# First layer of a two-layer trunk: low parts of k written by VectorE, last values projected ahead of the last queries

## The chip, the core and the metric

One core of a Trainium2 chip runs the whole program. The metric is the device time of one execution in microseconds (us). The engines are TensorE (PE, with its weight loads as PEld), VectorE (DVE), ScalarE (ACT) and GpSimd (POOL); SyncE (SP) issues the DMAs.

## The reference, cut to what matters

The trunk has two layers on 512 tokens of width 1024, in float32. Layer 0 mixes with stick-breaking attention, layer 1 with dilated attention; each layer then has a feed-forward block and a gated addition (PLE). Only the first mixer is touched by the change:

```python
q, k, v = jnp.split(x @ w_in, 3, axis=-1)          # 16 heads of 64
for blk in range(S // Q_BLOCK):                      # blocks of 128 queries
    z = einsum('bqhd,bkhd->bhqk', q[:, t0:L], k[:, :L]) * scale
    log_fail = where(past, log_sigmoid(-z), 0.0)
    later = cumsum(log_fail, reverse=True) - log_fail
    a = where(past, exp(log_sigmoid(z) + later), 0.0)
    outs.append(einsum('bhqk,bkhd->bqhd', a, v[:, :L]))
return concatenate(outs) @ w_out
```

## The kernel before

**Precision.** Every product is made of single-pass fp32r matmuls. A value is split into a high part (ScalarE rounds it by a copy) and a low part (VectorE subtracts), and high x high, high x low and low x high are summed. Weights arrive as units of 128 x 1024 (`Weights`, L64 to L118); ScalarE (L100), or GpSimd for every second unit from 6 to 28 (L98), makes the high part and VectorE (L101) the low part.

**Heads.** A pair `pr` of heads (two heads of 64 features) is projected by `queries(pr)` (L466): eight steps of three matmuls for q into one PSUM bank, eight for k into another. `query_part` scales each out of PSUM (L462: `qf`, then `kf`), and after `kf` calls `heads_split` (L368). For head a that makes `qa` (high part of q in partitions 0 to 63, low part in 64 to 127), `ka` (the high part of k in both halves) and `la` (the low part of k in both halves); `qb`, `kb`, `lb` are the same for head b. So one matmul `ka` by `qa` and one `la` by `qa` give all products.

For pairs 2 to 7 (`moved`) whole tiles are split (`qh`, `ql`, `kh`, `kl`: L380, L383, L386, L391), and twelve DMAs of 128 KB, issued one after the other by SP (`move`, L375), carry the halves to their places. For pairs 0 and 1 the engines write the halves themselves, except that the second half of `la` and of `lb` is a copy of the first by DMA (L406).

**Attention of one head n** (0 to 15; `pr = n // 2`). `stage1(n)` (L471) makes the scores in PSUM tile `z` and starts the logarithms on ScalarE and VectorE; its first matmul reads `ka` and `qa` (L478), its third reads `la` (L485). `stage2(n)` (L510) adds the running sums with `sh`, `sl`, `Lh`, `Ll` and starts the exponential `e`, `eh`, `el`. `stage3(n)` (L530) multiplies by the values. There are two `z` tiles and two further PSUM banks (`mm`) for all projections, `stage3` and PLE tiles.

**Order of the work.** TensorE's order is the order in which the program is written; the other engines' orders are planned from priorities. Between the stages `Filler` (L123) deals out projection steps from a queue, each counted as 0.65 on its own clock. Its queue here is, before the change, q2, v1, q3, q4, q5, v2, q6, q7, v3 (`q` is a pair's queries and keys, `v` the values of four heads, 16 steps each, 144 in all), and behind them two PLE tiles of two steps each ("tail"). The loop over n is

```python
stage2(n); fill(share * 0.57)
fill.until(("q", (n + 2) // 2), 5.0)     # pair done, and 5.0 of other steps after it
stage1(n + 2); fill(share * 0.32)
fill.until(("v", n // 4), 0.0); settle(1.5); stage3(n)
if n == 12: fill.add("out3", ...)        # output projection, only now in the queue
fill(share * 0.11)
```

`until` (L149) runs steps until the label is done and the extra 5.0 have passed; if the queue runs empty it stops there. A step of values is six matmuls of 256 columns, one of queries three of 512.

Of the kernel before, what the change touches and what calls it, by code (L numbers as in the profile page):

```python
# [11 lines left out]
F32 = mybir.dt.float32  # L12
# [153 lines left out]
def program(tc, ctx, w_dram, x_dram, xs_dram, p_dram, pos_dram, g_dram, c_dram, out_dram):  # L166
    nc = tc.nc
    pe, act, dve, pool = nc.tensor, nc.scalar, nc.vector, nc.gpsimd
# [10 lines left out]
    def U(name, dt=F32):  # L179
        return up.tile([P, T], dt, name=name, tag="u")  # L180

    def tmp(name, dt=F32):
        return tp.tile([P, T], dt, name=name, tag="tmp")
# [39 lines left out]
    def due(what):  # L223

        return tc.high_priority(offset=-TUNE[what])
# [30 lines left out]
    HALF = (slice(0, 64), slice(64, 128))  # L256
# [108 lines left out]
                            evac(n, ps[n], ALL)  # L365
                    yield 0.65

    def heads_split(qf, kf, name, moved):  # L368


        qa, qb, ka, kb, la, lb = (U(name + s, F32R) for s in ("qa", "qb", "ka", "kb", "la", "lb"))
        a, b = HALF

        def move(dst, src):
            nc.sync.dma_start(dst.bitcast(F32), src.bitcast(F32))  # L375

        with due("hsplit"):
            if moved:
                qh, ql, kh = tmp("qh", F32R), qf.bitcast(F32R), tmp("kh", F32R)
                act.activation(qh, qf, AF.Copy)  # L380
                move(qa[a], qh[a])
                move(qb[b], qh[b])
                dve.tensor_sub(ql, qf, qh.bitcast(F32))  # L383
                move(qa[b], ql[a])
                move(qb[a], ql[b])
                act.activation(kh, kf, AF.Copy)  # L386
                for h, t in ((a, ka), (b, kb)):
                    move(t[a], kh[h])
                    move(t[b], kh[h])
                kl = tmp("kl", F32R)  # L390
                dve.tensor_sub(kl, kf, kh.bitcast(F32))  # L391
                for h, t in ((a, la), (b, lb)):
                    move(t[a], kl[h])
                    move(t[b], kl[h])
            else:
                act.activation(qa[a], qf[a], AF.Copy)
                act.activation(qb[b], qf[b], AF.Copy)
                dve.tensor_sub(qa[b], qf[a], qa[a].bitcast(F32))
                dve.tensor_sub(qb[a], qf[b], qb[b].bitcast(F32))
                act.activation(ka[a], kf[a], AF.Copy)  # L400
                act.activation(kb[b], kf[b], AF.Copy)
                act.activation(ka[b], kf[a], AF.Copy)
                act.activation(kb[a], kf[b], AF.Copy)
                for h, t, k in ((a, la, ka), (b, lb, kb)):
                    dve.tensor_sub(t[h], kf[h], k[h].bitcast(F32))
                    move(t[HALF[1 - HALF.index(h)]], t[h])  # L406
        return (qa, qb), (ka, kb), (la, lb)


    def stick_breaking(xh, xl, sq, oh, ol, tail, tail_prepare, out):  # L410
        with tc.tile_pool(name="sbw", bufs=1, reuse_waits="tile") as wp, \
                tc.tile_pool(name="sbz", bufs=2, space=PSUM, reuse_waits="tile") as zp:
            seg = {0: (0, 512), 1: (512, 384), 3: (896, 128), 2: (1024, 256)}
            vt, norm, qk, live = {}, {}, {}, {}
# [10 lines left out]
            def value_part(qv, t, ps):  # L425
                norm["read"] = fill.clock + 0.65
                c = norm["col"][:, t:t + 1]
                v = wp.tile([P, 4, 2, 64], F32R, name="v", tag="v", bufs=8)
                with due("vev"):
                    src = ps[:, (t % 2) * 256:(t % 2) * 256 + 256].rearrange("p (h d) -> p h d", h=4)  # L430
                    hi, lo = v[:, :, 0], v[:, :, 1]
                    act.activation(hi, src, AF.Copy, scale=c)
                    dve.scalar_tensor_tensor(lo, src, c, hi.bitcast(F32), ALU.mult, ALU.subtract)
                vt[qv, t] = v

            def values(qv):
                w = []
                for t0 in (0, 2):
                    ps = bank()
                    for k in range(KT):  # L440
                        if t0 == 0:
                            w.append(W.take("w_in_sb", k, 2048 + qv * 256, 256))
                        for t in (t0, t0 + 1):
                            value_step(ps, k, t, *w[k])
                        if k == KT - 1:
                            value_part(qv, t0, ps)
                            value_part(qv, t0 + 1, ps)
                        yield 0.65
# [9 lines left out]
            def query_part(pr, f, m, ps):  # L458
                norm["read"] = fill.clock + 0.65
                f[m] = tmp("qf" if m == 0 else "kf")  # L460
                with due("qev"):
                    dve.tensor_mul(f[m], ps, norm["row8"] if m == 0 else norm["row"])  # L462
                if m == 1:
                    qk[pr] = heads_split(f[0], f[1], f"sb{pr}", pr > 1)

            def queries(pr):  # L466
                f = {}
                yield from linear("w_in_sb", [pr * P, 1024 + pr * P], xh, xl,
                                  lambda m, ps, cs: query_part(pr, f, m, ps), bank)
# [94 lines left out]
            for pr in range(2):  # L564
                f = {}
                for m in range(2):
                    query_part(pr, f, m, cols[2 * pr + m])
            for t in range(4):
                value_part(0, t, vps[t // 2])
            for name, n in (("q", 2), ("v", 1), ("q", 3), ("q", 4), ("q", 5), ("v", 2), ("q", 6), ("q", 7),  # L570
                            ("v", 3)):
                fill.add((name, n), queries(n) if name == "q" else values(n))
            fill.done.update({("q", 0): 0.0, ("q", 1): 0.0, ("v", 0): 0.0})
            fill(TUNE["p0"])
# [383 lines left out]
    def layer(i, h, xh, xl, sq, last):  # L958
# [44 lines left out]
        if i == 0:  # L1003
            stick_breaking(xh, xl, sq, oh, ol, [ple_tile(m, bank, U) for m in range(2)], ple_parts, out)
            later["pool"] = ctx.enter_context(tc.tile_pool(name="wide", bufs=6, space=PSUM, reuse_waits="tile"))
        else:
            outs = {}
            dilated(xh, xl, sq, oh, ol, outs, out, ple_parts)
# [158 lines left out]
    h, xh, xl, s = layer(0, xs_dram, xh, xl, s, False)  # L1167
# [45 lines left out]
```

## Time and profile before

| | |
|---|---|
| median of 3 runs | 1430.84 us (1430.02 to 1432.11) |
| the profiled execution | 1431.45 us, span 1429.3 us |
| PE busy | 1401.6 us, 98% of the span |
| DVE, ACT busy | 899.3 us (63%), 643.4 us (45%) |
| chain that ended last | PE 87%, DVE 7%, ACT 4%, issue 1%, DMA 1% |
| layer 0 attention, us 40 to 240 | DVE 15 to 18.5 and ACT 16 to 18 of each 20 us until 200, less after |

The span is the time between the first and last instruction of the profiled execution; its own time is 2.15 us longer. A row of the timeline gives start and duration in us, engine, line, operation and tiles; in square brackets stands the idle time of the engine just before and what ended it. Matmuls overlap, so the distance of two starts is the cost of one, not the duration.

### The profile page before, as it was taken

The page shows a single profiled execution, that of the slowest core. Times are in us where ns is not written, and L with a number is a line of the kernel's source. Part 1 is how long each engine was busy: PE and PEld are TensorE (multiplying, and loading weights), DVE is VectorE, ACT ScalarE, POOL GpSimd, SP SyncE. Part 2 cuts the span into 40 slices and gives each one's busy share as a digit, 9 for nine tenths or more (in the row PEclk, how much of TensorE's full clock was granted, in tenths as well). Part 3 has the DMA queues.
Part 4 walks back from the last instruction along what each step waited for, and adds up shares of the span by engine and source line. Part 5 has one row for each costly group of instructions (what it writes and reads, how often), then busy time and mean ns, then how long its engine had stood idle before and what let it go on. Part 6 is the DMA issues. An engine that isn't in the chain of part 4 may idle for free.

```text
span 1429.3 us, 18374 instructions
## 1 busy us (share of the span) xinstructions
PE 1401.6 (98%) x7218; PEld 1181.3 (83%) x7218; DVE 899.3 (63%) x1503; ACT 643.4 (45%) x1010; POOL 46.1 (3%) x27
## 2 busy tenths in 40 slices
PE   8999999999999999999999999999999999999998
PEld 7888997888888888887988788899888888888877
DVE  4788886485253453548868888866872444535476
ACT  4788986553232221335552525546632322222353
POOL 0111111000000000000000000000000000000000
PEclk9999999999999999999999999999999999999999
DMA  6344452423232323232522212132323333323321
GB/s 207 104 110 120 111 135 67 138 89 103 89 103 89 103 89 102 90 94 73 167 74 89 74 45 75 59 105 88 89 89 101 91 103 89 102 90 96 96 83 65
DMA packets 45270, 138.86 MB, mean 97 GB/s; under 512 B 5696, under 2 KB 6592, under 8 KB 45184
## 3 DMA queue, kind: packets, MB, share of 16 engines
q1 hardware_dynamic: 45104, 137.43, 31.9%
q8 instruction: 57, 0.93, 0.3%
q0 software_dynamic: 80, 0.26, 0.1%
q14 instruction: 29, 0.24, 0.1%
HBM read 123.51 MB, written 4.19 MB: 89 GB/s over the span
## 4 chain that ended last, share of the span: by engine, by line
PE 87%; DVE 7%; ACT 4%; issue 1%; DMA 1%; SPq 0%; ACTq 0%; DVEq 0%
PE wb L358 17%; PE wb L360 17%; PE wb L362 17%; PE mmb L358 5%; PE mmb L362 5%; PE mmb L360 5%; ACT S L774 1%; DVE wlo L101 1%; PE mmb L421 1%; PE mmb L422 1%; PE mmb L423 1%; PE wb L725 1%; PE z L261 1%; PE z L259 1%; PE z L260 1%
## 5 line engine op out<-in xcount | busy, mean ns | idle before, releaser
L100 ACT ACTIVATE whi<-wraw_t 128x1024 fp32r<-128x1024 f32 (+1 forms) x298 | 228.9, 798 | 440.6 <-PE wb L362 345.7
L101 DVE TENSOR_TENSOR wlo<-wraw_t,whi 128x1024 fp32r<-128x1024 f32 (+1 forms) x310 | 276.1, 911 | 238.7 <-ACT whi L100 235.5
L358 PE MATMUL wb<-nh,whi 128*128 128x512 f32 (+1 forms) x594 | 227.4, 385 | 4.4 <-ACT nh L264 4.4
L360 PE MATMUL wb<-nh,wlo 128*128 128x512 f32 (+1 forms) x594 | 226.4, 384 | 0.0
L362 PE MATMUL wb<-nl,whi 128*128 128x512 f32 x576 | 207.7, 391 | 0.4 <-DVE nl L268 0.4
L358 PE MATMUL wb<-fh,whi 128*128 128x512 f32 x496 | 196.5, 396 | 0.0
L360 PE MATMUL wb<-fh,wlo 128*128 128x512 f32 x496 | 196.5, 396 | 0.0
L362 PE MATMUL wb<-fl,whi 128*128 128x512 f32 x496 | 196.5, 396 | 0.0
L358 PEld LDWEIGHTS wb<-nh,whi 128*128 128x128 f32 x594 | 111.7, 188 | 28.8 <-ACT nh L264 7.0
L360 PEld LDWEIGHTS wb<-nh,wlo 128*128 128x128 f32 x594 | 111.7, 188 | 21.6
L362 PEld LDWEIGHTS wb<-nl,whi 128*128 128x128 f32 x576 | 107.8, 188 | 23.3 <-DVE nl L268 1.3
L362 PEld LDWEIGHTS wb<-fl,whi 128*128 128x128 f32 x496 | 93.3, 188 | 22.4
L358 PEld LDWEIGHTS wb<-fh,whi 128*128 128x128 f32 x496 | 93.3, 188 | 22.4
L360 PEld LDWEIGHTS wb<-fh,wlo 128*128 128x128 f32 x496 | 93.3, 188 | 22.4
L358 PE MATMUL mmb<-nh,whi 128*128 128x512 f32 x248 | 100.1, 404 | 0.0
L362 PE MATMUL mmb<-nl,whi 128*128 128x512 f32 x248 | 97.4, 393 | 0.0
L360 PE MATMUL mmb<-nh,wlo 128*128 128x512 f32 x248 | 97.3, 392 | 0.0
L1103 DVE TENSOR_TENSOR f<-wb,f 128x512 f32<-128x512 f32 (+1 forms) x50 | 33.3, 666 | 73.5 <-PE wb L362 71.1
L1078 DVE TENSOR_TENSOR z<-wb,rrow 128x512 f32<-128x512 f32 x60 | 40.5, 686 | 55.8 <-PE wb L362 55.7
L1081 ACT ACTIVATE fh<-z 128x512 fp32r<-128x512 f32 x64 | 39.9, 631 | 77.3 <-DVE z L1079 77.3
L291 DVE TENSOR_TENSOR acc<-acc,sq 128x512 f32<-128x512 f32 (+1 forms) x74 | 48.8, 659 | 15.6 <-ACT sq L287 15.0
L362 PEld LDWEIGHTS mmb<-nl,whi 128*128 128x128 f32 x248 | 46.9, 189 | 10.2
(818 smaller groups left out, 2600.8 us busy)
## 6 DMA issues: line engine op xcount, KB each, us to landing
wraw_t<-w SPq DMA_DIRECT2D x219, 512.0 KB, 3.6
x<-x SPq DMA_DIRECT2D x8, 256.0 KB, 7.1
h<-xs SPq DMA_DIRECT2D x8, 256.0 KB, 5.9
spill<-h SPq DMA_DIRECT2D x8, 256.0 KB, 2.7
h<-spill SPq DMA_DIRECT2D x8, 256.0 KB, 6.5
out<-h SPq DMA_DIRECT2D x7, 256.0 KB, 2.1
praw<-p SPq DMA_DIRECT2D x4, 256.0 KB, 4.2
wraw_t<-w SPq DMA_DIRECT2D x4, 128.0 KB, 3.5
```

The source lines that it names most:

```text
L100: self.highs.append(self.nc.scalar.activation(hi[:, c], src[:, c], AF.Copy))
L101: self.lows.append(self.nc.vector.tensor_sub(lo[:, c], src[:, c], hi[:, c].bitcast(F32)))
L259: pe.matmul(ps, ah, bh, start=start, stop=False, skip_group_check=True)
L260: pe.matmul(ps, ah, bl, start=False, stop=False, skip_group_check=True)
L261: pe.matmul(ps, al, bh, start=False, stop=stop, skip_group_check=True)
L291: self.adder.tensor_tensor(self.acc[:, cs], self.acc[:, cs], self.sq[:, cs], ALU.add)
L358: pe.matmul(ps[m][:, cs], wh, xh[k][:, cs], start=(k == 0 and cs is not TWO[1]), stop=False, skip_group_check=True)
L360: pe.matmul(ps[m][:, cs], wl, xh[k][:, cs], start=False, stop=False, skip_group_check=True)
L362: pe.matmul(ps[m], wh, xl[k], start=False, stop=(k == nk - 1), skip_group_check=True)
L1078: dve.tensor_mul(z, ps, norm["row"])
L1081: act.activation(a, z, AF.Copy)
L1103: dve.tensor_add(y[m][:, cs], ps, y[m][:, cs])
```

## The change

Two edits. For pair 0 VectorE subtracts a second time, straight into the other half of `la` and `lb`, where a DMA copied it. In the Filler's queue the last values (v3) stand ahead of the last pair of queries (q7). Pair 1 keeps its DMAs; nothing else differs.

```diff
-    def heads_split(qf, kf, name, moved):
+    def heads_split(qf, kf, name, moved, at_once):
...
                 for h, t, k in ((a, la, ka), (b, lb, kb)):
                     dve.tensor_sub(t[h], kf[h], k[h].bitcast(F32))
-                    move(t[HALF[1 - HALF.index(h)]], t[h])
+                    other = HALF[1 - HALF.index(h)]
+                    if at_once:
+                        dve.tensor_sub(t[other], kf[h], k[h].bitcast(F32))
+                    else:
+                        move(t[other], t[h])
...
-                    qk[pr] = heads_split(f[0], f[1], f"sb{pr}", pr > 1)
+                    qk[pr] = heads_split(f[0], f[1], f"sb{pr}", pr > 1, pr == 0)
...
-            for name, n in (("q", 2), ("v", 1), ("q", 3), ("q", 4), ("q", 5), ("v", 2), ("q", 6), ("q", 7),
-                            ("v", 3)):
+            for name, n in (("q", 2), ("v", 1), ("q", 3), ("q", 4), ("q", 5), ("v", 2), ("q", 6), ("v", 3),
+                            ("q", 7)):
```

## Rows read from the trace of the kernel before

**Rows 1.** The page, part 1: busy us, share of span, instructions.

```profile
PE 1401.6 (98%) x7218; PEld 1181.3 (83%) x7218; DVE 899.3 (63%) x1503; ACT 643.4 (45%) x1010; POOL 46.1 (3%) x27
```

**Rows 2.** Timeline of PE, first scores of head 0: start, us, instruction, idle.

```profile
51.50 0.39 PE L478 MATMUL z<-sb0qa,sb0ka 128*128 128x512 f32 x1
51.73 0.22 PE L480 MATMUL z<-rconst 128*128 128x128 f32 x1
53.01 0.47 PE L485 MATMUL z<-sb0qa,sb0la 128*128 128x512 f32 x1 [1.06 <-DMA sb0la<-sb0la]
```

**Rows 3.** Timeline of DVE around the low parts of pair 0.

```profile
49.92 0.68 DVE L405 TENSOR_TENSOR sb0la<-kf,sb0ka 64x512 fp32r<-64x512 f32 x1
...
51.36 1.23 DVE L101 TENSOR_TENSOR wlo<-wraw_t,whi 128x1024 fp32r<-128x1024 f32 x1
...
58.99 1.49 DVE L498 SCALAR_TENSOR_TENSOR s<-z,s 128x1280 f32<-128x1280 f32 x1 [1.68 <-ACT s L497]
```

**Rows 4.** Timeline of PE: PLE tiles, stages 3(12), 2(13), 1(15).

```profile
213.91 0.40 PE L358 MATMUL mmb<-ph,whi 128*128 128x512 f32 x1
...
214.61 0.40 PE L358 MATMUL mmb<-ph,whi 128*128 128x512 f32 x1
...
216.78 0.47 PE L358 MATMUL mmb<-ph,whi 128*128 128x512 f32 x1 [1.31 <-DVE v L433]
...
217.81 0.51 PE L538 MATMUL mmb<-eh,v 128*128 128x512 f32 x1
...
219.14 0.44 PE L513 MATMUL z<-sh,rconst 128*128 128x512 f32 x1
...
221.16 0.40 PE L358 MATMUL mmb<-ph,whi 128*128 128x512 f32 x1
...
223.24 0.47 PE L478 MATMUL z<-sb7qb,sb7kb 128*128 128x512 f32 x1
...
224.87 0.45 PE L259 MATMUL out<-o2h,whi 128*128 128x512 f32 x1
```

**Rows 5.** Timeline of PE: first matmul after keys of pairs 2, 6, 7; pair 6 used.

```profile
61.47 0.28 PE L421 MATMUL mmb<-whi,x0h 128*128 128x256 f32 x1
...
176.29 0.40 PE L358 MATMUL mmb<-x0h,whi 128*128 128x512 f32 x1
...
186.50 0.47 PE L485 MATMUL z<-sb6qa,sb6la 128*128 128x512 f32 x1 [0.32 <-DMA sb6la<-kl]
...
195.94 0.28 PE L421 MATMUL mmb<-whi,x0h 128*128 128x256 f32 x1
```

**Rows 6.** View by tile, sb2la and sb7la: DMA issues, first and last start; landing.

```profile
L375 SPq DMA_DIRECT2D sb2la<-kl x2: 540/571/602, 70.3 to 70.9; - x2
...
L375 SPq DMA_DIRECT2D sb7la<-kl x2: 539/563/587, 202.5 to 203.1; - x2
DMA to landing us min/median/max: 2.3/2.4/2.4
```

**Rows 7.** Timeline of DVE: q of pair 7 leaves PSUM.

```profile
185.70 0.68 DVE L462 TENSOR_TENSOR qf<-mmb,row 128x512 f32<-128x512 f32 x1
```

**Rows 8.** Timeline of ACT and SP: pair 7's split begins.

```profile
196.53 0.62 ACT L380 ACTIVATE qh<-qf 128x512 fp32r<-128x512 f32 x1
...
197.17 0.47 SPq L375 DMA_DIRECT2D sb7qa<-qh  x1
```

**Rows 9.** Windows: us, busy of PE, PEld, DVE, ACT, POOL, then granted clock.

```profile
716.00:720.00 4.00, 2.24 (x15) 1.95 (x15) 3.32 (x6) 4.00 (x6) 0.00 (x0) 0.90 0.16 20
720.00:724.00 4.00, 4.00 (x19) 4.00 (x20) 2.72 (x7) 1.72 (x4) 1.83 (x1) 0.50 0.28 111
214.00:218.00 4.00, 2.59 (x11) 1.54 (x10) 1.67 (x3) 3.64 (x5) 2.77 (x1) 1.00 0.35 121
218.00:222.00 4.00, 4.00 (x24) 3.60 (x24) 3.41 (x8) 1.96 (x3) 0.00 (x0) 1.00 0.23 55
```

**Rows 10.** Timeline of DVE: last low part of head 15's sums.

```profile
236.45 0.82 DVE L507 TENSOR_TENSOR Ll<-L,Lh 128x640 fp32r<-128x640 f32 x1
```

## The prediction

> **What bounds the kernel.** I read the page first: TensorE is busy for 98% of the span, no other engine comes near [rows 1], and the chain of waits is TensorE's own work for the most part. So what counts is where TensorE stands still. The list of its waits gives few; in the stretch that the change touches they are short, and the timeline shows each in its place. Three matter. Head 0's first matmul with a low part of k waits 1.06 us for the DMA that copies it [rows 2]. Head 12's waits 0.32 us for a DMA of pair 6 [rows 5]. The second PLE tile waits 1.31 us for VectorE to clear the bank of the last values [rows 4]. A fourth, at about 231 us, is head 14's exponential; it follows stage 2 of head 14 in either order and is left as it is. Then I followed pair 7 from its last key matmul to its use, because that pair is the one moved.
>
> **Edit 1, pair 0.** Removed: two DMAs of SP. Added: two subtractions of 64x512 on VectorE at 0.68 us each, the price of the same operation into the first half [rows 3]. `la` is then complete at 49.92 + 2 x 0.7 = 51.3 us, ahead of 51.9, when TensorE wants it after the two matmuls that precede it [rows 2]. The wait of 1.06 us goes: **-1.1 us**. The ends: 0, if VectorE's plan puts other work between the two halves, and -1.2: the starts stand 1.28 us apart, and 128 columns need a quarter of the 0.23 us that the 512-column matmul ahead took. The added 1.4 us of VectorE push what is queued behind it: the low part of a weight unit at 51.36, then pair 1's split and an eviction. The first to notice would be the logarithm step at 58.99, and VectorE stood idle for 1.68 us before that one, waiting for ScalarE [rows 3]; that idle time covers the 1.4. Without that cover it would cost at most the 1.4. On SP the weight load behind the two copies waits for that same low part, so it starts 1.4 us later; it fetches a unit needed much later. I take 0.
>
> **Edit 2, what it removes.** The queue order decides which 16 steps come last. Stage 2 of head 12 starts after 135 of the 144 steps in either order, since every step counts 0.65 and no `until` before it asks for v3 or q7. Before, the nine left are values: five, stage 1 of head 14, four more, then three PLE steps, the third after the bank wait. That wait vanishes, for the bank is then pair 7's and is cleared by the multiply of L462, planned early, while the first PLE tile runs. From 213.91 two steps at 0.70 end at 215.3, the third began at 216.78 [rows 4]: **-1.5 us** (0 if the multiply is late by two steps). Pair 6 is now followed by nine steps of values before its use, six short matmuls each instead of three long ones and so a little longer; the 0.32 us shrinks: **-0.2 us** (0 to -0.3, the whole wait).
>
> **Edit 2, what it adds.** Stage 1 of head 14 needs pair 7. The nine steps left after stage 2 of head 12 are now pair 7's own, so `until` runs all nine, and then asks for 5.0 of other steps. The queue holds four PLE steps (2.6) and nothing more: the output projection joins it only behind stage 3 of head 12. So `until` stops, and stage 1 of head 14 stands four steps after the last key matmul. On the chip that is 4 x 0.70 = 2.8 us [rows 4], plus 0.4 for the two matmuls ahead of the one that reads `la` [rows 2]: 3.2 us.
>
> What pair 7 needs in that time: `kf` out of PSUM, the rounding on ScalarE, the subtraction on VectorE, and twelve DMAs one behind the other on SP, the tenth of which completes `la`. The trace has this path six times. For pair 7 the keys end at 195.94, the second `la` DMA is issued at 203.1 and lands 2.4 us later: 9.6 us [rows 5, 6]. For pair 6 TensorE itself waited, 10.2 us after the keys [rows 5]. The longest is pair 2: 70.9 + 2.4 - 61.47 = 11.8 us [rows 5, 6]. I take 9.6, the nearest row: the same pair, at a time when ScalarE and VectorE will have less to do than they had then, because TensorE feeds them nothing new. TensorE is in order, and behind the waiting matmul stand stage 3 of head 12, stage 2 of head 13 and the output projection, which could all have run. So it stands still for 9.6 - 3.2 = **+6.4 us** (+8.6 with pair 2's length, +3.8 in the second rival).
>
> **After the stall.** Stage 2 of head 14 now follows its stage 1 by stage 3(12) and stage 2(13), 3.35 us from 217.81 to 221.16, four steps (2.8), stage 1(15) (1.63), two steps (1.4) and stage 3(13) (1.33): 10.5 us [rows 4]. Head 15's last low part was ready at 237.27, 12.4 us after its stage 1 ended at 224.87 [rows 4, 10], and it is read in the last quarter of stage 2, some 1.5 of the 2.0 us from 219.14 to 221.16; so 10.9 is wanted and 10.5 there. I take this as even (0 to +1.5).
>
> **The clock.** Where TensorE was busy for 2.24 of 4 us, the granted clock fell to 0.50 for the next 4 us (1.2 GHz instead of 2.4); around the 1.31 us wait, busy 2.59 of 4, it stayed at 1.00 [rows 9]. A stall of 6.4 us, broken only by two matmuls, is much worse than the first. Four microseconds at half clock lose 2 us: **+2.0 us** (0 to +4, a fall twice as long). What the lower clock loses in stage 1 and 3 is time that ScalarE and VectorE gain for head 14, so it and the term above do not add up in full.
>
> The Trainium skill's page "TensorE: Matmul & The Clock Gate", section "Part 1: The HAM clock gate (the "warmup" mystery)", says that "the default state is throttled, and activity releases the throttle". By that rule the edit costs more than the stall itself, and the sum would hold the clock term; a reading of the 1.31 us wait alone would leave it out. Rows 9 show both outcomes.
>
> **Sum.** -1.1 - 1.5 - 0.2 + 6.4 + 2.0 = +5.6 us. On the profiled execution's 1431.45 that is 1437.05; that execution is 0.61 above the median of the runs shown, and on the median it is 1436.4. I predict 1436.5. Nothing later gives it back, since TensorE bounds the rest too.
>
> **Rivals.**
> - *The stall without the fall of the clock*: +3.6, so 1434.4. For it: no fall after 1.31 us. Against: the fall shown by rows 9 after far less idle time.
> - *The split starts early.* q of pair 7 leaves PSUM long before its keys end. If its rounding and four q DMAs went ahead then, SP would start with k: `kf`, rounding and six DMAs at 0.6, landing at about 7.0, a stall of 3.8 and no fall: +1.0, 1431.9. Against: before, `qf` was there at 185.70, yet `qh` began at 196.53 and the first DMA at 197.17, both after the last key matmul, before 195.94 [rows 5, 7, 8]; the other five pairs show the same order.
> - *Covered: not slower.* If `la` of pair 7 lands within 3.2 us of the keys, the stall is nothing and only the gains stand: -2.8, 1428.0. That decides at one point, the matmul of stage 1 of head 14 that reads `la`. Against: two landings in a row cannot be beaten; 2.4 us of 3.2 are one DMA's landing alone [rows 6].
> - *Pile-up.* The path takes pair 2's 11.8 us, or the clock stays down twice as long, with heads 13 to 15 now bunched on ScalarE: +8 to +10, about 1440. For it: three heads' chains follow one stall.
> - *Edit 1 does nothing*, because the second half of `la` is planned behind the weight unit: 1.1 more on any of these; it moves the time within the range only.
>
> **How the numbers follow.** Forecast 60%, no fall 12%, early split 9%, covered 6%, pile-up 13%. The range is 1432 to 1441: it reaches from the early split to the pile-up's end and leaves out the covered case and what lies beyond a +10. A measurement of this kernel can tell about 0.2%, 2.9 us, from no change; slower by that means above 1433.7. Forecast, no fall and pile-up lie there: 85%. The early split and half of the covered case lie within: 12%. Faster: 3%.
>
> **What would show it.** In the changed kernel's timeline: the first `la` matmul of head 0 under 0.2 us after the one before; no wait of a PLE tile for values; stage 1 of head 14 behind four PLE steps, its first matmul waiting about 4 us for a DMA of `sb7ka` and its third again about 2 us for `sb7la`; a granted clock of 0.50 within a few us of it. The prediction is wrong if those waits together are under 3 us, if TensorE has other steps ahead of stage 1 of head 14, or if head 14's stage 2 waits for longer than 3 us.

## The result, and the profile after

The changed kernel takes 1443.43 us (median of 4 runs, 1442.68 to 1444.0), the kernel before 1431.47 beside it: ratio 1.0083 [1.0066, 1.01], +12.0 us. Forecast were 1436.5 and a range of 1432 to 1441. The sign came as forecast, and so did the stall that was to cause it; the size did not. The profiled execution took 1443.91, 12.46 more than that of before; its span is 12.5 longer. Of the eleven runs of e6 below one took 2801.06 us, for a reason that no run here shows, and it is left out of e6's figures.

The page, part 1: every engine is busy as before within 0.5%, so the 12 us are time in which TensorE stands still or runs slower.

```profile
PE 1407.3 (98%) x7218; PEld 1184.9 (82%) x7218; DVE 901.4 (63%) x1505; ACT 643.3 (45%) x1010; POOL 45.9 (3%) x27
```

To see where, lay the two timelines of PE side by side at instructions that both have. First the kernel after (line numbers beyond L407 are 4 higher than before):

```profile
51.72 0.44 PE L489 MATMUL z<-sb0qa,sb0la 128*128 128x512 f32 x1
...
68.10 0.39 PE L523 MATMUL z<-Ll,minus_r 128*128 128x256 f32 x1 [0.55 <-DVE Ll L511]
...
202.73 0.47 PE L542 MATMUL mmb<-eh,v 128*128 128x512 f32 x1 [0.84 <-DVE v L437]
...
212.91 0.39 PE L358 MATMUL mmb<-ph,whi 128*128 128x512 f32 x1
...
214.31 0.50 PE L358 MATMUL mmb<-ph,whi 128*128 128x512 f32 x1
...
215.59 0.39 PE L362 MATMUL mmb<-pl,whi 128*128 128x512 f32 x1
220.59 0.77 PE L482 MATMUL z<-sb7qa,sb7ka 128*128 128x512 f32 x1 [4.61 <-DMA sb7ka<-kh]
...
222.43 0.76 PE L489 MATMUL z<-sb7qa,sb7la 128*128 128x512 f32 x1 [0.96 <-DMA sb7la<-kl]
...
224.80 0.73 PE L542 MATMUL mmb<-eh,v 128*128 128x512 f32 x1
...
227.15 0.52 PE L517 MATMUL z<-sh,rconst 128*128 128x512 f32 x1
...
236.24 0.44 PE L517 MATMUL z<-sh,rconst 128*128 128x512 f32 x1
...
241.18 0.80 PE L259 MATMUL z<-o0h,whi 128*128 128x512 f32 x1 [2.76 <-ACT e L528]
...
244.34 0.40 PE L260 MATMUL z<-o0l,whi 128*128 128x512 f32 x1
...
250.86 0.39 PE L542 MATMUL mmb<-eh,v 128*128 128x512 f32 x1
...
729.30 1.86 PE L303 MATMUL mmb<-mean,natural 128*128 128x1 f32 x8 [1.30 <-DVE natural L299]
...
739.28 0.51 PE L666 MATMUL mmb<-whi,uh 128*128 128x512 f32 x1 [1.43 <-DVE rrow L322]
...
875.86 0.66 PE L761 MATMUL wb<-consts,m 2*128 2x2 f32 x8
```

and those of the kernel before that answer to them and do not stand in [rows 2, 4]:

```profile
209.42 0.40 PE L478 MATMUL z<-sb7qa,sb7ka 128*128 128x512 f32 x1
...
210.99 0.34 PE L421 MATMUL mmb<-whi,x4h 128*128 128x256 f32 x1
...
228.97 0.39 PE L513 MATMUL z<-sh,rconst 128*128 128x512 f32 x1
...
232.42 0.50 PE L259 MATMUL z<-o0h,whi 128*128 128x512 f32 x1 [1.33 <-ACT e L524]
...
234.14 0.39 PE L260 MATMUL z<-o0l,whi 128*128 128x512 f32 x1
...
719.17 1.87 PE L303 MATMUL mmb<-mean,natural 128*128 128x1 f32 x8 [1.28 <-DVE natural L299]
...
727.94 0.50 PE L662 MATMUL mmb<-whi,uh 128*128 128x512 f32 x1
...
863.27 0.65 PE L757 MATMUL wb<-consts,m 2*128 2x2 f32 x8
```

Where the order differs, one compares like with like: at the PLE tile the kernel before has done stage 1 of head 14 already, 1.57 us (209.42 to 210.99), and at stage 3(12) the kernel after has done one PLE step more (0.69).

| place | after minus before, us | what came in between |
|---|---|---|
| head 0's first `la` matmul | -1.29 | pair 0's DMA is gone |
| stage 2(0), last quarter | -0.63 | wait for `Ll`, 0.55 and the refill |
| first PLE step | 212.91 - (213.91 - 1.57) = +0.57 | wait for `v` at stage 3(11) and small ones |
| third PLE step | 214.31 - (216.78 - 1.57) = -0.90 | the PLE wait of 1.31 is gone |
| stage 3(12) | 6.99 - 0.69 = +6.30 | stall for pair 7, clock |
| stage 2(14) | +7.27 | stage 3(12) at half clock |
| first output matmul | +8.76 | wait for `e(14)`, 2.76 for 1.33 |
| its eighth | +10.20 | the clock fell again |
| end of layer 0 | +10.13 | nothing in 485 us |
| entry of layer 1 | +11.34 | wait for `rrow`, 1.43 |
| some 136 us later | +12.59 | a longer fall of the clock (+11.02 at the wait just ahead of it, 843.19 before and 854.21 after) |

The windows view of the kernel after (stretch; busy us of PE, PEld, DVE, ACT, POOL; granted clock) shows the two falls at 220 and 241, each from the end of a stall of TensorE on:

```profile
216.00:220.00 4.00, 0.00 (x0) 0.00 (x0) 1.22 (x1) 0.60 (x1) 0.28 (x1) 1.00 0.94 212
220.00:222.00 2.00, 0.87 (x2) 0.50 (x2) 0.00 (x0) 0.00 (x0) 0.00 (x0) 0.61 0.89 214
222.00:224.00 2.00, 1.57 (x6) 1.51 (x6) 0.00 (x0) 0.00 (x0) 0.00 (x0) 0.50 0.90 224
224.00:226.00 2.00, 2.00 (x9) 1.81 (x8) 0.00 (x0) 0.96 (x1) 0.00 (x0) 0.50 0.30 115
226.00:228.00 2.00, 2.00 (x10) 1.86 (x10) 0.00 (x0) 1.94 (x3) 0.00 (x0) 0.68 0.00 0
...
236.00:240.00 4.00, 2.42 (x16) 1.93 (x15) 2.05 (x3) 3.53 (x5) 0.00 (x0) 1.00 0.46 131
240.00:242.00 2.00, 0.82 (x2) 0.72 (x3) 1.93 (x4) 1.97 (x4) 0.00 (x0) 0.73 0.00 0
242.00:244.00 2.00, 2.00 (x6) 1.52 (x6) 2.00 (x5) 2.00 (x3) 0.00 (x0) 0.50 0.00 0
```

The stall itself is on SP's own timeline (compare [rows 6]): four pairs of k copies in a row, each pair 1.2 us, head b's between head a's. The first three pairs:

```profile
216.32 1.20 SPq L375 DMA_DIRECT2D sb7ka<-kh  x2
217.56 1.23 SPq L375 DMA_DIRECT2D sb7kb<-kh  x2
218.91 1.18 SPq L375 DMA_DIRECT2D sb7la<-kl  x2
```

And ScalarE's timeline shows why head 14's exponential is later. Its scores are ready when stage 2(14) ends (the last of its matmuls starts at 238.09 and lasts 0.33), but the logarithm of head 15 (L501) stands ahead of it:

```profile
238.75 1.25 ACT L501 ACTIVATE s<-s 128x1280 f32<-128x1280 f32 x1
239.91 1.22 ACT L528 ACTIVATE e<-z 128x1280 f32<-128x1280 f32 x1
```

### The profile page after: what moved, and what is told of

The parts are those of the page before. It is cut to its first block, busy times and chain, and to the rows that moved or that the text cites. A ratio compares the mean times of both kernels' runs of the same rounds, so it can differ in the third digit from the quotient of the medians.

```text
span 1441.8 us, 18372 instructions
## 1 busy us (share of the span) xinstructions
PE 1407.3 (98%) x7218; PEld 1184.9 (82%) x7218; DVE 901.4 (63%) x1505; ACT 643.3 (45%) x1010; POOL 45.9 (3%) x27
## 4 chain that ended last, share of the span: by engine, by line
PE 86%; DVE 7%; ACT 4%; issue 1%; DMA 1%; SPq 0%; POOL 0%; ACTq 0%; DVEq 0%
PE wb L358 17%; PE wb L360 17%; PE wb L362 17%; PE mmb L358 5%; PE mmb L362 5%; PE mmb L360 5%; DVE wlo L101 1%; ACT S L778 1%; PE wb L729 1%; PE z L261 1%; PE z L259 1%; PE wb L824 1%; PE mmb L425 1%; PE z L260 1%; PE mmb L426 1%
```

## The experiments

All times stand against runs of the kernel before on the same chip (medians 1430.87 for the first four, 1431.02 for the next four, 1430.94 for the last). "After" is the changed kernel, 1443.43, beside which the kernel before took 1431.47; so a difference "against after" is good to about half a microsecond. Single profiles differ by up to some 3 us in when layer 0 gets going (see the last section), so shifts are read between landmarks of one profile, or with the difference at the wait for `Ll` in stage 2(0) taken off ("start taken off").

**e1, the low parts alone** (after, with the old queue order):

```diff
-            for name, n in (("q", 2), ("v", 1), ("q", 3), ("q", 4), ("q", 5), ("v", 2), ("q", 6), ("v", 3),
-                            ("q", 7)):
+            for name, n in (("q", 2), ("v", 1), ("q", 3), ("q", 4), ("q", 5), ("v", 2), ("q", 6), ("q", 7),
+                            ("v", 3)):
```

> Edit 1 alone, queue order as before. Theory (all of the loss comes from pair 7's split, which the new order leaves uncovered): faster than before by 0.6 us, 1430.9 against 1431.5: the 1.3 us of head 0's wait gone, 0.6 given back where stage 2 of head 0 waits for VectorE's last low part (Ll). Rival (the added VectorE work is what costs, by delaying the chains of a stretch in which VectorE is over 80% busy): slower by 1 us or more, with more waits of TensorE for VectorE between 55 and 110 us than the one at 68 us.

Measured 1429.76 (11 runs), 0.9994 [0.9985, 1.0003]. In its profile TensorE is 1.06 us early at head 0 and 0.40 early after stage 2(0), where it waits 0.54 us for `Ll`. The edit does what it says, gives part of it back 16 us later, and cannot be told from no change in the times.

**e2, the order alone** (before, with v3 ahead of q7):

> Edit 2 alone, pair 0 copied by DMA as before. Theory: slower than before by 12.5 us, 1444, as the changed kernel plus the 0.6 us that edit 1 is worth; TensorE waits 4.6 and 1.0 us for DMAs of pair 7. Rival (VectorE's added work shares in the loss): slower by less than 10 us.

Measured 1444.56 (4 runs), 1.0093 [1.0076, 1.0109]; waits of 4.86 for `sb7ka`, 0.86 for `sb7la`, 2.75 for `e(14)`. The order makes the whole loss.

**e3, pair 7's wait taken away** (after; pair 7 is split by the engines as pair 0 is, without DMAs):

```diff
-  heads_split(f[0], f[1], f"sb{pr}", pr > 1, pr == 0)
+  heads_split(f[0], f[1], f"sb{pr}", 1 < pr < 7, pr in (0, 7))
```

> The changed kernel, with pair 7 split as pair 0 is, by ScalarE and VectorE straight into place, without its twelve DMAs. Theory (the path from pair 7's keys to its use is twelve DMAs issued in a row): after the keys there are the k eviction, six ScalarE halves of 0.65 and the low parts, so the first matmul with the low part comes about 5 us after the keys instead of 9.5; the wait of 6.3 us falls to about 2, the clock falls for a shorter time or not at all, and the kernel is faster than the changed one by 5 to 8 us: 1435.5 to 1438.5. Rival (the wait is for the engines before the DMAs, the k eviction and the rounding, which stay): within 2 us of the changed kernel's 1443.4.

Measured 1434.0 (10 runs), 1.002 [1.001, 1.003]: -9.4 against after, more than expected. PE's timeline:

```profile
213.89 0.50 PE L358 MATMUL mmb<-ph,whi 128*128 128x512 f32 x1 [1.44 <-DVE kf L466]
...
215.86 0.50 PE L482 MATMUL z<-sb7qa,sb7ka 128*128 128x512 f32 x1 [0.32 <-ACT sb7ka L402]
216.26 0.44 PE L489 MATMUL z<-sb7qa,sb7la 128*128 128x512 f32 x1
```

`la` is used 5.3 us after the keys end (210.94) instead of 9.5, the wait is 0.32, and the clock holds 1.00 from 216 to 224. So the stall and what follows it are about three quarters of the loss; in the profiles, start taken off, e3 is 7.7 ahead of after at the end of layer 0 (of the 10.1 that after has lost there), and the rest of its gain is in layer 1. What is left costs 3.1: the PLE tile waits as before, now for `kf` (1.44 for 1.31), stage 3(11) waits 0.8 for `v`, and TensorE 2.3 for `e(14)`.

**e4, the stall filled with work** (after; 40 matmuls of 256 columns into columns of `z` that nobody reads, ahead of stage 1 of head 14):

```diff
+                for _ in range(40 if n == 14 else 0):
+                    pe.matmul(z[:, 1280:1536], ident_r, rconst[:, 0:2 * P], start=True, stop=True, ...)
```

> The changed kernel with 40 matmuls of 256 columns put ahead of stage 1 of head 14, into columns of its score tile that nothing reads; they fill 4.7 us of the time in which TensorE stands still. Theory (the fall of the clock to 1.2 GHz costs 2.1 us of its own in stages 1 and 3 behind the stall): the clock stays at 1.00 through stage 3 of head 12 and the kernel is 2 us faster than the changed one, 1441.4; if the later fall at 241 us goes too, 1439.9. Rival (the clock's loss is hidden, since ScalarE and VectorE set the pace behind the stall): 1443.4, no change, or slower by what the dummies push.

Measured 1438.02 (4 runs), 1.0048 [1.0033, 1.0063]: -5.4 against after, where -2 to -3.5 was expected. The granted clock is 1.00 from 212 to 228. From the first matmul that reads `la` to stage 2(13) e4 takes 2.57 us (221.43 to 224.00), after 4.72 (222.43 to 227.15): the clock's first fall costs 2.15. The rest of the 5.4 is later: the wait for `e(14)` is 2.24 (2.76 in after), and in layer 1 the wait for `rrow` is 0.2 instead of 1.4 and the fall of the clock behind the wait for `kl` half as long.

**e6, one subtraction less** (e1, with the second half of `lb` copied by DMA again), to see why `Ll` is late:

```diff
-                    if at_once:
+                    if at_once and h is a:
```

> Order as before; VectorE writes the second half of la alone, lb is copied by DMA as before. Theory (of edit 1's 1.06 to 1.3 us gain, 0.66 comes back at stage 2 of head 0, because VectorE's two added subtractions make the last low part Ll late): with one subtraction instead of two the wait at 68 us shrinks or goes, and the kernel is 0.3 to 0.6 us faster than with edit 1 alone: 1429.3. Rival (Ll is late for the order in which VectorE's work was planned, not for the 0.7 us): no difference from 1429.8.

Measured 1429.57 (ten runs), 0.9989 [0.998, 0.9998]. `Ll` is as late (the wait is 0.54 again). VectorE's timeline names what stands ahead of it: the low part of a weight unit, as in e1 and after.

```profile
63.70 1.21 DVE L101 TENSOR_TENSOR wlo<-wraw_t,whi 128x1024 fp32r<-128x1024 f32 x1
64.83 0.81 DVE L511 TENSOR_TENSOR Ll<-L,Lh 128x640 fp32r<-128x640 f32 x1
```

So it is not the volume of the added subtractions that makes `Ll` late; the planned order behind them is what is left. e6 is the fastest version that was run, 1.45 us under the kernel before; the upper end of its interval lies barely under 1, and e1 cannot be told from it.

**e8, head 14's exponential first** (after; the logarithm of head 15 is held until `e(14)` has been issued on ScalarE):

```diff
...
+                        i = act.activation(s, s, AF.Ln, bias=1.0)
+                        if n == 15:
+                            after(i, live["exp"])
...
```

> The changed kernel with head 15's logarithm put behind head 14's exponential on ScalarE. Theory (behind the stall heads 13 to 15 are bunched on ScalarE, so the exponential of head 14 starts 1.5 us after its stage 2 has ended, and the 2.76 us that the output projection waits for it bring the clock down a second time): the wait falls to about 1.4 us, the second fall of the clock goes, and the kernel is 2 to 3 us faster than the changed one: 1440.4 to 1441.4. Rival (head 15's stage 2 then waits for the logarithm instead): within 1 us of 1443.4, with a new wait of stage 2 of head 15.

Measured 1440.6 (4 runs), 1.0065 [1.005, 1.0081]: -2.8 against after. PE's timeline, and a window of the same profile (busy us of PE, clock):

```profile
240.18 0.50 PE L259 MATMUL z<-o0h,whi 128*128 128x512 f32 x1 [1.60 <-ACT e L538]
```

```profile
240.00:244.00 4.00, 3.82 (x17) 1.00 0.00 0
```

The wait is 1.16 shorter than in after, and the second fall of the clock is gone. From stage 3(13) to the eighth output matmul e8 takes 6.74 us (235.17 to 241.91), after 9.32 (235.02 to 244.34): one instruction's place on ScalarE is worth 2.6 there. But the rival came as well: head 15's logarithm is late now, its stage 2 waits 0.22 for `sl` and 0.43 for `Ll`, and from the eighth output matmul to stage 3(14) e8 takes 7.69 us (to 249.60), after 6.52 (to 250.86). So 1.2 of the 2.6 goes back. That the times still differ by 2.8 has other sources, which no run ties to this edit: the wait for `ka` is 0.4 shorter (4.20), and 1.0 is gained at the entry of layer 1, where a fall of the clock is half as long (see the last section).

**e9, more cover behind pair 7's keys** (after; four steps of the output projection enter the queue earlier):

```diff
...
+                if n == 12:
+                    outs = {}
+                    fill.add("out3", early_out(outs))
...
-                if n == 12:
-                    outs = {3: bank("out")}
-                    fill.add("out3", out(outs, (3,), range(6)))
```

> The changed kernel with the first part of the output projection in the queue before the loop's round of head 12, so that four more steps stand between pair 7's keys and stage 1 of head 14. Theory (the wait is 9.5 us less what TensorE has to do meanwhile): the wait for la falls by 4 x 0.69 = 2.8 us, from 6.3 to 3.5. But those steps are then missing between stage 1 and stage 2 of head 14, where its logarithms need about 10 us, so part of it comes back there: 1440.6 to 1443. Rival (cover is all that is missing, nothing comes back): 1440.6 or less, no wait of stage 2 of head 14.

Measured 1440.3 (4 runs), 1.0067 [1.0053, 1.0081]: -3.1 against after.

```profile
221.34 0.47 PE L482 MATMUL z<-sb7qa,sb7ka 128*128 128x512 f32 x1 [1.53 <-DMA sb7ka<-kh]
...
223.13 0.77 PE L489 MATMUL z<-sb7qa,sb7la 128*128 128x512 f32 x1 [1.26 <-DMA sb7la<-kl]
...
251.36 0.39 PE L542 MATMUL mmb<-eh,v 128*128 128x512 f32 x1
```

The two waits fall from 5.57 to 2.79, which is the four steps of 0.70. Most of that comes back, as the theory had it and by more than it said: TensorE now waits 0.42 at stage 1(15) for `e`, 0.30 in stage 2(14) for `sl`, and 2.93 for `e(14)`. At stage 3(14) e9 stands at 251.36 and after at 250.86; start taken off (1.11), e9 is 0.6 early there, and 0.7 at the end of layer 0. Most of the 3.1 comes from the entry of layer 1: from the wait for `natural` to that for `rrow` e9 takes 8.03 us (729.75 to 737.78), after 9.98 (729.30 to 739.28), with the same shorter fall of the clock as e8. The time alone would have spoken for the rival; in layer 0 more cover was worth less than one microsecond.

**e10, a shorter path** (after; for pair 7 head a's six DMAs go ahead of head b's):

```diff
+                    row(qa[a], qh[a])
+                    row(qa[b], ql[a])
+                    for t, s in ((ka, kh), (la, kl)):
+                        row(t[a], s[a])
+                        row(t[b], s[a])
...
```

> The changed kernel with pair 7's twelve DMAs in another order: the six of head a first, then the six of head b, so that the second la DMA is the sixth instead of the tenth. Theory (the path is as long as the row of DMAs on SP, 0.62 us each): la lands 2.5 us earlier, about 7 us after the keys, the waits of stage 1 of head 14 fall by as much, and the kernel is 2.5 us faster than the changed one, 1440.9. Rival (the path is the engines' work and one DMA's landing): no change, 1443.4.

Measured 1436.44 (4 runs), 1.0038 [1.0025, 1.0052]: -7.0 against after, where -2.5 was expected. SP's and PE's timelines:

```profile
217.22 1.19 SPq L389 DMA_DIRECT2D sb7la<-kl  x2
```

```profile
220.34 0.50 PE L514 MATMUL z<-sb7qa,sb7la 128*128 128x512 f32 x1 [0.77 <-DMA sb7la<-kl]
```

`la` is issued sixth on SP, used 7.2 us after the keys (213.16) and not 9.5. The direct gain is 2.3, close to the forecast. At stage 3(14) (246.71) e10 is 4.4 ahead of after, start taken off (0.26): TensorE waits 1.6 for `e(14)`, and the second fall is gone. But the plan of ScalarE has changed too: `e(14)` (236.02) stands ahead of head 15's logarithm (237.14), as e8 forced it, and what of the added gain is owed to the shorter stall and what to that order no run separates. The other 2.6 come at the entry of layer 1 (7.36 us from `natural` to `rrow`, 725.13 to 732.49, where after takes 9.98): the shorter fall of the clock again, and 0.2 of wait for `rrow`.

**e11, one instruction of layer 1** (after; the copy of `rrow` goes ahead of the weight's low part on VectorE, as before):

```diff
...
+            after(W.lows[mark], sq.copied)
...
```

> The changed kernel with one order fixed: at the entry of layer 1 the copy of the norm's row (L322, rrow) is made to go ahead of the weight unit's low part on VectorE, as it does in the kernel before. In the changed kernel that copy stands behind the 1.22 us low part, and TensorE waits 1.43 us at 739.28 for the bank that the copy frees; in the kernel before it does not wait there. Theory A (the changed plan of VectorE's work reaches layer 1 and costs the wait there): the wait falls to 0.3 us or less and the time falls by 1.0 to 1.4 us against the changed kernel, to 1442.0 to 1442.4; TensorE's shift against the kernel before is 10 us at both ends of the entry of layer 1, instead of 10.1 and 11.3. Rival B (the clock makes it: the shift of 1.2 comes with the longer fall at 728 to 736, and the wait only fills it): the wait goes but the shift stays at 11 or more, and the time stays at 1443.4. Either way the second fall of the clock in layer 1 (3.4 us long before, 6.8 after) may come out as 0, 3.4 or 6.8 us, and that moves the time by up to 3.4 us by itself; the shift at the entry, not the time, tells A from B.

Measured 1441.16 (5 runs), 1.0069 [1.0056, 1.0083]: -2.3 against after. In after VectorE does

```profile
737.41 1.22 DVE L101 TENSOR_TENSOR wlo<-wraw_t,whi 128x1024 fp32r<-128x1024 f32 x1
738.54 0.68 DVE L322 COPY rrow<-mmb 128x512 f32<-128x512 f32 x1
```

In e11 the matmul waits 0.32 at 735.77, and TensorE's shift against before is 7.75 at 724.58 (before 716.83) and 7.83 at 735.77 (before 727.94), where after falls another 1.2 behind between them. So the wait is the plan's and not the clock's. The rest of the 2.3 is within what the fall behind the wait for `kl` moves (here 3.4 us long, 6.8 in after).

## Why the prediction came out as it did

**Edit 1, -1.1: right in place, half of it given back.** `la` is complete in time and TensorE gains 1.29, 0.07 of which it had ahead of the edit. The idle 1.68 us of VectorE at 58.99 [rows 3] did hide the subtractions (0.30 are left of it). But I asked only who is pushed back, not whether the plan of VectorE changes: a weight unit's low part came ahead of `Ll(0)`, and 0.66 went back. The sum had taken that at nothing.

**What edit 2 removes, -1.7: right at the PLE tile, not on balance.** The PLE wait and pair 6's are gone. The wait for the last values did not vanish, though: it stands at stage 3(11) now, 0.84, because `v` again follows a weight's low part on VectorE (200.98, then 202.11); no run puts that order back, so its price is read from the trace alone. Net of both edits TensorE is 0.90 early at the third PLE step, where the sum had 2.8: this term was 1.9 too large.

**The stall, +6.4: right.** Stage 1 of head 14 stands behind four PLE steps; `la` is used 9.5 us after the keys (212.91 to 222.43; 9.6 predicted) and the delay is 6.2 (216.2, where `la` would have been read, to 222.43). The landing took 2.9 us instead of 2.4, and the issue came that much earlier.

**Stage 2 of head 14, "even": right.** It does not wait.

**The clock, +2.0: right for the fall I counted, in part by luck.** e4 puts it at 2.15. But the 2.0 came from one stretch of 4 us at 0.50, and the fall in [rows 9] was longer; the stretch behind it, in the kernel before, reads

```profile
724.00:728.00 4.00, 3.92 (x24) 3.44 (x22) 3.48 (x9) 2.96 (x7) 0.00 (x0) 0.75 0.00 0
```

so that (0.10 + 0.50 + 0.25) x 4 = 3.4 us of clock were lost there. After loses as much from 220 to 228, (0.39 + 0.50 + 0.50 + 0.32) x 2 = 3.4, and pays 2.15, as TensorE stood still for part of it (busy for 0.87 and 1.57 us of the first two stretches of 2). The prediction cited the Trainium skill, "TensorE: Matmul & The Clock Gate", "Part 1: The HAM clock gate (the "warmup" mystery)", that the throttled clock is the default. The rows agree (0.50 behind the stall), and the rule would have had me ask the same at each further wait that grows.

**What failed** first is the sentence on the wait at 231 us, a term that the sum put at nothing: "it follows stage 2 of head 14 in either order and is left as it is". It follows the same stage, but stage 1 of head 15 now comes late, so that head's logarithm is ready on ScalarE just ahead of `e(14)`. The wait grew from 1.33 to 2.76 (+1.5 in the table), and behind it the clock fell a second time (+1.4): 2.9 that the sum did not hold. e8 takes 2.6 of it away by that one order, at 1.2 for head 15. This is what the pile-up rival had ("heads 13 to 15 now bunched on ScalarE"), at 13%. Its other form, that "the clock stays down twice as long", did not add to the cost of the first fall; the clock fell twice.

**The other miss is layer 1**, about 2.4 us. "Nothing later gives it back" held, but later added: 1.2 through the place of one copy on VectorE (e11), and 1.25 net between that point and the last landmark, where a fall of the clock some 115 us on costs 1.6 more than before and 0.3 come back ahead of it. The first is the plan of an engine that neither edit touches there. No run ties the second to an edit; it stays open. In a sum, the three terms that were mis-sized or put at nothing: 5.6 + 1.9 (less gained ahead of the stall: 2.8 - 0.9) + 2.9 + 2.4 = 12.8, where 12.5 was measured; the stall was 0.2 under its term. The range's upper end, +10, had room for the largest of the three, not for all of them.

**The rivals.** "Covered" at 1428.0 was wrong twice: e3 takes the stall away almost wholly and still stands at 1434.0. "The split starts early" came for one copy only: the first of `qh` was issued at 212.64, ahead of the keys' end at 212.91, but the k copies started at 216.32. "The stall without the fall of the clock" did not come: 0.50.

## What to carry to other kernels

A stall moved or added is priced three times: by its own length, by a possible fall of the clock behind it, and by each wait behind it that it lengthens; go through those waits one by one, above all where two heads' chains now reach ScalarE together. Where other engines' orders are planned, an edit can put a 1.2 us filler ahead of a 0.5 us step that somebody waits for, hundreds of microseconds away; three such swaps cost 0.7, 0.8 and 1.2 us here, the last of them shown by undoing it (e11). An experiment's time can agree with a theory by chance: in e9 the stall's gain had mostly gone back before layer 1, and another stretch made up for it. When a path of queued copies binds, order the queue by first use (e10: one head's six of the twelve copies first, 2.3 us directly).

## What the runs showed of the hardware that was not expected

**One wait, three falls.** In layer 1 the same wait of 1.92 us for `kl` (at 843.19 before, at 854.21 after) is followed by a clock that differs from kernel to kernel though TensorE's work is the same. The windows view from the wait on, of after and of e1:

```profile
852.00:856.00 4.00, 2.08 (x26) 1.82 (x27) 4.00 (x5) 1.01 (x1) 0.00 (x0) 0.92 0.02 4
856.00:860.00 4.00, 4.00 (x15) 3.42 (x15) 2.65 (x19) 0.00 (x0) 0.00 (x0) 0.50 0.43 131
860.00:864.00 4.00, 4.00 (x19) 3.58 (x18) 1.39 (x2) 0.70 (x2) 0.00 (x0) 0.73 0.00 0
```

```profile
840.00:844.00 4.00, 2.08 (x27) 1.61 (x26) 3.63 (x6) 1.25 (x2) 0.00 (x0) 1.00 0.00 0
844.00:848.00 4.00, 4.00 (x26) 3.59 (x27) 3.11 (x20) 0.59 (x1) 0.00 (x0) 1.00 0.46 135
```

PE is busy for the same 2.08 of the first 4 us in both. After loses (0.08 + 0.50 + 0.27) x 4 = 3.4 us there, as do e2, e8, e9 and e10; e1 and e6 lose nothing, and before, e3, e4 and e11 half, 1.7. So this wait was followed by a loss of 0, 1.7 or 3.4 us of clock, and no run shows what decides between them. The entry of layer 1 is alike: around the wait of 1.3 us for `natural` the clock loses 3.4 us in before, after, e1, e2, e3, e4, e6 and e11 and 1.7 in e8, e9 and e10. Nor does a wait's length settle it: behind 2.25 us for `e(14)` in e3 the clock holds 1.00 (232 to 240), behind 2.24 in e4 it falls (0.76, then 0.81, from 236 to 244). So e8 and e10 show their second fall gone beside a shorter wait, not that the length of the wait alone took it away.

**The start is not fixed.** The first matmul that waits long for a weight (L259, 0.9 to 3.1 us) began between 10.22 us (e6) and 12.00 us (e8) in the profiled executions, with the same work ahead of it; at the wait for `Ll` in stage 2(0) e11 and e9, whose layer 0 has the same program up to there, stand at 66.20 and 69.21; and the ten runs of e3 spread from 1430.8 to 1435.6. A difference of a few microseconds is read from the shift between landmarks, not from two times.
